# Gate and up of two experts in chunks of 1024 columns instead of 512

## The chip, the core and the metric

The kernel runs on one core of one Trainium2 chip. The metric is the time of one execution on the device in microseconds. On the core, TensorE (PE in the profile) multiplies matrices, VectorE (DVE) and ScalarE (ACT) do the elementwise work, GpSimd (POOL) does a little of it, and SyncE (SP) issues nearly all transfers from memory; 16 DMA engines carry them. Each engine works through its own queue in order.

## What is computed

A trunk of two layers over 256 tokens of width 1024 in float32: attention in three groups of heads, then a dense SwiGLU in the first layer and eight experts, two for each token, in the second. The change concerns the experts alone:

```python
logits = xf @ w_router
top_logit, top_idx = lax.top_k(logits, 2)
gates = softmax(top_logit)
# for each token and each of its two experts e:
y = (silu(x @ w_gate[e]) * (x @ w_up[e])) @ w_down[e]
out = h + sum of gates * y
```

w_gate and w_up of an expert are 1024 x 3584, w_down is 3584 x 1024: 44.0 MB for each expert, 352 MB for all eight. Every expert's weights are read once.

## The kernel before

The first 500 us or so are attention, the dense layer and the router. Then the experts run. The kernel counts the tokens of each expert and sorts experts 1 to 7 by count; expert 0 keeps its place. When all but three have at most 32 tokens, as here, the path `woven()` runs. It holds two streams:

- **Heavy (H):** three experts whose weights are split on the way, since a product in float32 is made of three products in a faster format. ACT makes the high part of a group of weights (`whi`, line 124), DVE the rest (`wlo`, line 125), and `mm3` (lines 238 to 240) multiplies high by high, high by low and low by high. Expert 0 and the expert with place 2 in the order have up to 128 tokens, one tile: `large_one` does these two, and the change is in there. The expert with place 1 has two tiles: `large_two`, lines 1348 to 1350.
- **Small (S):** five experts with at most 32 tokens each. TensorE multiplies their weights as they are (lines 1442 for gate and up, 1464 for down). A group is one row block of 1792 columns (896 KB) or two rows of down (1024 KB); an expert has 32 groups of the first kind and 14 of the second, 46 in all.

A heavy group is 512 KB: [128, 2, 512] of gate or up, which is two rows of 2 KB on each of 128 partitions, or [128, 1, 1024] of down, one row of 4 KB. Gate and up are cut into seven chunks of 512 columns. Each chunk takes four groups of gate, four of up, and then four groups of down of the chunk before; `turn` transposes the chunk's product of 512 columns through one PSUM bank (line 1290), and ACT and DVE split the result (lines 1293 and 1294). One expert has 84 heavy groups.

A string `order` fixes in which order the groups of the two streams are loaded and used: some 30 heavy groups are loaded before `woven()` starts, and then 0.3 small groups go beside each heavy group of the one-tile experts, and 2.1 beside each of the two-tile expert. `fill()` issues the loads on SP (line 79) in this order whenever a raw buffer is free. A heavy group frees its raw buffer when its split is done, a small group when its matmuls are done. There are five slots for split weights; `LOOK = 3` says how far ahead in the order the splits are issued.

In PSUM, `gu` has two banks: gate of a chunk goes to the first, up to the second. ACT reads gate for SiLU (line 1312), DVE multiplies it with up (line 1310). `wide_y` holds the sums of down. One bank, `tr`, serves all transposes and gathers. `jobs` is a list of small pieces of work (one-hot matrices, gathers, adding an expert's result back); one is taken after each group of the order. In chunk `NCH - 2`, the last but one, the gather of the next expert's rows is hung on this list: `gather`, lines 845 to 880, whose one-hot matrix lies in the tile `ph`, of which there is one. `gather_few` (lines 1405 and 1410) does the same for a small expert through the same tile. The instructions of each engine are put in order by a scheduler when the kernel is built, so the order in the trace is not line by line that of the code.

Of the kernel before, what the change touches and what calls it, by code (L numbers as in the profile page):

```python
# [8 lines left out]
F32 = mybir.dt.float32  # L9
# [3 lines left out]
AF = mybir.ActivationFunctionType  # L13
ALU = mybir.AluOpType
# [4 lines left out]
KT = D // 128  # L19
# [21 lines left out]
def encoder_kernel(ctx: ExitStack, tc: tile.TileContext, a: dict, consts: bass.AP, out: bass.AP):  # L41
    nc = tc.nc
# [15 lines left out]
    groups = []  # L58
# [5 lines left out]
    pos_ = {"dma": 0, "split": 0, "use": 0, "end": 1 << 30, "most": 1 << 30, "large": False}  # L64
# [131 lines left out]
    n_dense = len(groups)  # L196
    def expert_groups(e, chunks, pairs=False, by_columns=False):


        wg, wu = ([v.rearrange("e (k p) n -> p (e k) n", p=128) for v in (a[nm][0, bass.ds(e, 1)],)][0]  # L200
                  for nm in ("w_gate_moe", "w_up_moe"))
        wd = a["w_down_moe"][0, bass.ds(e, 1)].rearrange("e (k p) n -> p (e k) n", p=128)
        res = []
        for i, c in enumerate(chunks):
            c0 = c * 512
            ks = range(0, KT, 2)
            order = [(w, k) for k in ks for w in (wg, wu)] if pairs else [(w, k) for w in (wg, wu) for k in ks]
            both = [w[:, k:k + 2, c0:c0 + 512] for w, k in order]
            before, this = ([wd[:, k:k + 1, :] for k in range(4 * b, 4 * b + 4)] for b in (c - 1, c))
            last = c == chunks[-1]  # L210
            if by_columns and last:
                this = [wd[:, 4 * c:4 * c + 4, k:k + 256] for k in range(0, D, 256)]
                both, before = before, both
            res += both + (before if i else []) + (this if last else [])
        return res

    def wide_groups(e, parts, by_columns=False):


        wg, wu = (a[nm][0, bass.ds(e, 1)].rearrange("e (k p) n -> p (e k) n", p=128)  # L220
                  for nm in ("w_gate_moe", "w_up_moe"))
        wd = a["w_down_moe"][0, bass.ds(e, 1)].rearrange("e (c p r) n -> p (e c) r n", p=128, r=WR)
        res = []
        for c in parts:
            res += [w[:, k:k + 1, c * WIDE:(c + 1) * WIDE] for k in range(KT) for w in (wg, wu)]
            ends = WR - 4 if by_columns and c == parts[-1] else WR
            res += [wd[:, c, r:r + 2, :] for r in range(0, ends, 2)]
            if ends < WR:
                res += [wd[:, c, ends:, k:k + 256] for k in range(0, D, 256)]
        return res  # L230

    WIDE, WR = DFE // 2, DFE // 256
    NCH = DFE // 512
    groups += expert_groups(0, list(range(NCH)))

    def mm3(ps, xs, ws, start, stop):
        (xh, xl), (wh, wl) = xs, ws
        nc.tensor.matmul(ps, xh, wh, start=start, stop=False)  # L238
        nc.tensor.matmul(ps, xh, wl, start=False, stop=False)  # L239
        return nc.tensor.matmul(ps, xl, wh, start=False, stop=stop).ins  # L240
# [29 lines left out]
    def gcol(base, l, k):  # L270
        return gt[:, base + 8 * l + k:base + 8 * l + k + 1]
# [434 lines left out]
    def moe():  # L706
        with ExitStack() as st:
            mp = st.enter_context(tc.tile_pool(name="moe", bufs=1, reuse_waits="tile"))
# [58 lines left out]
            for k in range(KT):  # L767
# [3 lines left out]
                d, g = hTs[k // 4][:, k % 4, :], gcol(G_FFN, 1, k)  # L771
# [147 lines left out]
            for t in range(NT):  # L919
                last = nc.scalar.activation(gate[:, t, :], gate[:, t, :], AF.Exp, scale=rs[:, t:t + 1])  # L920
# [177 lines left out]
            def result():  # L1098
                y = psum.tile([128, 2, 512], F32, name="y", bufs=1)
                return [y[:, q, :] for q in range(2)]  # L1100
# [113 lines left out]
            def woven():  # L1214
# [5 lines left out]
                        released(i)  # L1220
                loaded = pos_["dma"]
                few = [7, 6, 5, 3, 4]
                heavy = groups[n_dense:n_dense + 24 * NCH] + [g for c in every for g in expert_groups(ids[0], [c])]
                assert pos_["use"] == n_dense
                small = [g for e in few for g in wide_groups(ids[e - 1], [0, 1], e == few[-1])]
                order = "H" * (loaded - pos_["use"])
                n_h, n_s, due = len(order), 0, 0.0
                while n_h < len(heavy):
                    due += 0.3 if n_h < 24 * NCH else 2.1
                    order += "H"  # L1230
                    n_h += 1
                    while due >= 1.0:
                        order += "S"
                        n_s += 1
                        due -= 1.0
# [6 lines left out]
                n_split, n_used = [pos_["split"] - base], [0]  # L1242
                ready = dict(spl)

                def split_next():
                    i = n_split[0]
                    pos_["split"] = at[i]
                    hi, lo = split_into(at[i], slots[(at[0] - n_dense + i) % len(slots)])
                    ready[at[i]] = hi, lo
                    n_split[0] += 1  # L1250

                def take_heavy():
                    i = pos_["use"]
                    assert order[i - base] == "H"
                    while i not in ready:
                        split_next()
                    pos_["use"] += 1
                    return ready.pop(i)
# [9 lines left out]
                gu = [psum.tile([128, 512], F32, name="gu", bufs=2) for _ in range(2)]  # L1268
                wide_y = result()
                fixed.append(bank)  # L1270
                n, m = WIDE // 4, 256
# [11 lines left out]
                def large_one(col, slot, after):  # L1283

                    x, ths = xs[slot], None

                    def turn(hc):
                        pt = tr().rearrange("p (f c) -> p f c", f=4)
                        for f in range(4):
                            nc.tensor.transpose(pt[:, f, :], hc[:, f * 128:(f + 1) * 128], ident)  # L1290
                        th = mp.tile([128, 4, 128], F32R, name="th", bufs=2)
                        tl = mp.tile([128, 4, 128], F32R, name="tl", bufs=2)
                        nc.scalar.activation(th, pt, AF.Copy)
                        nc.vector.tensor_tensor(tl, pt, th.bitcast(F32), op=ALU.subtract)
                        return th, tl

                    for c in [*every, NCH]:
                        if c < NCH:
                            hc = mp.tile([128, 512], F32, name="sg", bufs=2)
                            for v in range(2):  # L1300
                                for kg in range(4):
                                    yield
                                    w = take_heavy()
                                    for k in range(2):
                                        kk = kg * 2 + k
                                        mm3(gu[v], (x[0][:, kk, :], x[1][:, kk, :]), (w[0][:, k, :], w[1][:, k, :]),
                                            kk == 0, kk == KT - 1)
                                    n_used[0] += 1
                                if v:
                                    nc.vector.tensor_tensor(hc, gu[v], hc, op=ALU.mult)  # L1310
                                else:
                                    nc.scalar.activation(hc, gu[v], AF.Silu)
                            if c == 1:
                                jobs.append(lambda: turn_hot(one_hot(col, cm[:, :128]), phTs[slot]))
                            if c == NCH - 2:
                                jobs.extend(after)
                        if c:
                            for f in range(4):
                                yield
                                wh, wl = take_heavy()  # L1320
                                for q in range(2):
                                    sl = slice(q * 512, q * 512 + 512)
                                    mm3(wide_y[q], (ths[0][:, f, :], ths[1][:, f, :]), (wh[:, 0, sl], wl[:, 0, sl]),
                                        c == 1 and f == 0, c == NCH and f == 3)
                                n_used[0] += 1
                        if c < NCH:
                            ths = turn(hc)
                    take(wide_y, spare(slot))
                    later_combine(col, slot, spare(slot))

# [195 lines left out]
            for dst, v in ((posS, pos), (gateS, gate)):  # L1526
# [3 lines left out]
            every = list(range(NCH))  # L1530
            ids = nc.values_load_multi_w_load_instructions(regs[0:1, 1:8], engines=[mybir.EngineType.SP],
                                                           min_val=0, max_val=NE - 1)[1]
# [158 lines left out]
```

## Time and profile before

| | us |
|---|---|
| median of 3 runs | 1404.87 (1404.04 to 1405.04) |
| the profiled execution | 1403.66 |
| its span, from first to last instruction | 1401.9 |
| PE busy | 1305.1 (93%) |
| DVE busy | 787.8 (56%) |
| ACT busy | 614.7 (44%) |

427.9 MB are moved, 305 GB/s over the span. Busy time of PE is modelled at its ends, since matmuls overlap; the start times are exact. The share of DMA is the mean busy share of the 16 engines; it can stand a little above 1, since a packet can begin before the last has ended. TensorE's clock is given as a share of full speed.

### The profile page before, as it was taken

To read this page: it belongs to the slowest core of one execution; us is meant where nothing else is said; L and a number is where in the kernel's file an instruction comes from. 1 tells how busy PE (TensorE), PEld (TensorE's weight loads), DVE (VectorE), ACT (ScalarE), POOL (GpSimd) and SP (SyncE) were. 2 spreads that over 40 slices of the span, in tenths; PEclk is the share of its full clock that TensorE was granted. 3 is DMA by queue.
4 is the path that set the end of the run, shared out by engine and by line. 5 is a ranking of instruction groups with operands and counts; after the bars stand their busy time and mean duration, and the time that the engine had idled before them with its cause. 6 is when DMAs were issued, how large, how long until landed. Compare 5 with 4: busy or idle time off the path is not lost.

```text
span 1401.9 us, 21803 instructions
## 1 busy us (share of the span) xinstructions
PE 1305.1 (93%) x8247; PEld 943.9 (67%) x8247; DVE 787.8 (56%) x1332; ACT 614.7 (44%) x951; POOL 70.2 (5%) x58
## 2 busy tenths in 40 slices
PE   8999999999999889999999989898999898989886
PEld 8886888888986567675666656565656566555642
DVE  7877877754986778675766553333332233233333
ACT  8576665643676556654555442212131212122211
POOL 0300011100300500000000000000000000000000
PEclk9999999999999999999999999999999999999999
DMA  8631555555654748999999987999999999999994
GB/s 269 188 120 64 178 181 180 185 193 163 209 173 151 267 164 306 377 405 375 379 402 403 357 327 293 361 411 415 410 416 410 416 411 414 412 414 413 413 418 163
DMA packets 146486, 427.87 MB, mean 305 GB/s; under 512 B 10412, under 2 KB 55860, under 8 KB 137668
## 3 DMA queue, kind: packets, MB, share of 16 engines
q1 hardware_dynamic: 146000, 425.62, 80.3%
q8 instruction: 66, 1.08, 0.3%
q0 software_dynamic: 288, 0.74, 0.2%
q14 instruction: 48, 0.39, 0.1%
q10 hardware_dynamic: 84, 0.04, 0.0%
HBM read 425.31 MB, written 1.05 MB: 304 GB/s over the span
## 4 chain that ended last, share of the span: by engine, by line
PE 66%; DMA 19%; DVE 9%; issue 2%; ACT 2%; POOL 1%; SPq 0%; ACTq 0%; DVEq 0%; POOLq 0%
DMA rawm<-in_w_down_moe_dram 8%; PE acc L652 6%; PE cb L1442 6%; PE y L239 3%; PE acc L238 3%; DMA room<-in_w_down_moe_dram 3%; PE acc L239 3%; PE acc L240 3%; PE y L238 3%; PE y L240 3%; PE gu L238 3%; PE acc L653 3%; PE gu L239 3%; PE gu L240 3%; PE tr L1464 3%; DVE wlo L125 2%
## 5 line engine op out<-in xcount | busy, mean ns | idle before, releaser
L140 DVE TENSOR_TENSOR wlo<-raw,whi 128x1024 fp32r<-128x1024 f32 (+2 forms) x134 | 149.0, 1115 | 58.2 <-ACT whi L139 58.0
L139 ACT ACTIVATE whi<-raw 128x1024 fp32r<-128x1024 f32 (+2 forms) x140 | 133.9, 966 | 75.2 <-PE acc L240 56.7
L125 DVE TENSOR_TENSOR wlo<-rawm,whi 128x1024 fp32r<-128x1024 f32 x87 | 104.8, 1220 | 68.6 <-ACT whi L124 68.6
L652 PE MATMUL acc<-u,whi 128*128 128x512 f32 x352 | 124.7, 399 | 0.0
L124 ACT ACTIVATE whi<-rawm 128x1024 fp32r<-128x1024 f32 x87 | 89.8, 1053 | 56.2 <-DMA rawm<-in_w_gate_moe_dram 19.3
L1349 PE MATMUL gu<-x,wlo 128*128 128x256 f32 x360 | 102.8, 290 | 10.8 <-DVE wlo L125 10.8
L1348 PE MATMUL gu<-x,whi 128*128 128x256 f32 x360 | 100.6, 296 | 5.3 <-ACT whi L124 5.3
L1350 PE MATMUL gu<-x,whi 128*128 128x256 f32 x360 | 100.7, 284 | 0.0
L653 PE MATMUL acc<-u,wlo 128*128 128x256 f32 x352 | 98.9, 281 | 0.0
L1348 PEld LDWEIGHTS gu<-x,whi 128*128 128x128 f32 x360 | 65.7, 190 | 31.6 <-issue 17.2
L238 PE MATMUL gu<-whi,x 128*128 128x512 f32 x178 | 73.7, 414 | 6.4 <-DVE regs L1525 4.6
L1349 PEld LDWEIGHTS gu<-x,wlo 128*128 128x128 f32 x360 | 68.5, 190 | 14.7 <-DVE wlo L125 13.7
L238 PE MATMUL acc<-whi,u 128*128 128x384 f32 (+1 forms) x224 | 75.4, 337 | 2.9 <-ACT qk_dil L566 2.9
L652 PEld LDWEIGHTS acc<-u,whi 128*128 128x128 f32 x352 | 66.2, 188 | 16.4
L240 PE MATMUL acc<-whi,u 128*128 128x384 f32 (+1 forms) x224 | 74.2, 331 | 0.0
L239 PE MATMUL acc<-wlo,u 128*128 128x384 f32 (+1 forms) x224 | 74.2, 331 | 0.0
L239 PE MATMUL gu<-wlo,x 128*128 128x512 f32 x178 | 72.2, 405 | 1.8 <-DVE wlo L125 1.6
L240 PE MATMUL gu<-whi,x 128*128 128x512 f32 x178 | 71.0, 399 | 0.0
L1350 PEld LDWEIGHTS gu<-x,whi 128*128 128x128 f32 x360 | 68.6, 191 | 0.5 <-issue 0.5
L1442 PE MATMUL cb<-rawm,room 128*32 128x448 f32 x528 | 67.1, 553 | 0.0
L653 PEld LDWEIGHTS acc<-u,wlo 128*128 128x128 f32 x352 | 66.5, 189 | 0.0
L125 DVE TENSOR_TENSOR wlo<-room,whi 128x1024 fp32r<-128x1024 f32 x25 | 30.5, 1222 | 45.3 <-ACT whi L124 45.3
(404 smaller groups left out, 2921.6 us busy)
## 6 DMA issues: line engine op xcount, KB each, us to landing
rawm<-in_w_up_moe_dram SPq DMA_DIRECT2D x35, 896.0 KB, 15.7
rawm<-in_w_gate_moe_dram SPq DMA_DIRECT2D x31, 896.0 KB, 14.9
rawm<-in_w_down_moe_dram SPq DMA_DIRECT2D x26, 1024.0 KB, 15.4
rawm<-in_w_down_moe_dram SPq DMA_DIRECT2D x48, 512.0 KB, 9.4
raw<-in_w_down_moe_dram SPq DMA_DIRECT2D x22, 1024.0 KB, 16.0
raw<-in_w_gate_moe_dram SPq DMA_DIRECT2D x23, 896.0 KB, 14.9
rawm<-in_w_up_moe_dram SPq DMA_DIRECT2D x36, 512.0 KB, 10.4
raw<-in_w_up_moe_dram SPq DMA_DIRECT2D x20, 896.0 KB, 15.7
```

What stands on the lines that cost most here:

```text
L125: nc.vector.tensor_tensor(xl, x, xh.bitcast(F32), op=ALU.subtract)
L139: nc.scalar.activation(xh, x, AF.Copy)
L140: (engine or nc.vector).tensor_tensor(xl, x, xh.bitcast(F32), op=ALU.subtract)
L238: nc.tensor.matmul(ps, xh, wh, start=start, stop=False)
L239: nc.tensor.matmul(ps, xh, wl, start=False, stop=False)
L240: return nc.tensor.matmul(ps, xl, wh, start=False, stop=stop).ins
L652: nc.tensor.matmul(ps, wh[:, k, fs], u[:, k], start=k == 0, stop=False)
L653: nc.tensor.matmul(ps[:, 0, :], wl[:, k, fs], uh[:, k, :], start=False, stop=k == KT - 1)
L1348: nc.tensor.matmul(o, wh, xh, start=kk == 0 and f % 2 == 0, stop=False)
L1349: nc.tensor.matmul(o, wl, xh, start=False, stop=False)
L1350: nc.tensor.matmul(o, wh, xl, start=False, stop=kk == KT - 1 and f % 2 == 1)
L1442: done = nc.tensor.matmul(ps[sub[j], :n], xr[:, k, :], v[:, 0, j * n:j * n + n], start=k == 0, stop=k == KT - 1)
```

## The change

The two one-tile experts take gate and up in chunks of up to 1024 columns. Expert 0 has its first three chunks as before, since their groups are loaded by the code in front of `woven()`, and then two of 1024; the other has three of 1024 and one of 512. A group of a wide chunk is [128, 1, 1024], one row of 4 KB on each partition, and covers one block of 128 rows of the contraction. Within a wide chunk, gate fills both `gu` banks (columns 0 to 511 and 512 to 1023), SiLU is taken from both, then up fills the same two banks. Down of a wide chunk takes eight groups. A wide chunk is transposed by two calls of `turn`. The gather of the next expert's rows is hung on the last chunk. The number of groups, their bytes and the order of H and S stay as they are.

```diff
+    def one_groups(e, chunks):
+        wg, wu, wd = (a[nm][0, bass.ds(e, 1)].rearrange("e (k p) n -> p (e k) n", p=128)
+                      for nm in ("w_gate_moe", "w_up_moe", "w_down_moe"))
+        res, last = [], []
+        for c0, n in chunks:
+            step = 1024 // n
+            res += [w[:, k:k + step, c0:c0 + n] for w in (wg, wu) for k in range(0, KT, step)] + last
+            last = [wd[:, k:k + 1, :] for k in range(c0 // 128, (c0 + n) // 128)]
+        return res + last
...
-                heavy = groups[n_dense:n_dense + 24 * NCH] + [g for c in every for g in expert_groups(ids[0], [c])]
-                assert pos_["use"] == n_dense
+                cut = {0: [(0, 512), (512, 512), (1024, 512), (1536, 1024), (2560, 1024)],
+                       2: [(0, 1024), (1024, 1024), (2048, 1024), (3072, 512)]}
+                heavy = one_groups(0, cut[0]) + one_groups(ids[1], cut[2])
+                n_one = len(heavy)
+                heavy += [g for c in every for g in expert_groups(ids[0], [c])]
+                assert pos_["use"] == n_dense and loaded <= n_dense + 36
...
-                    for c in [*every, NCH]:
-                        if c < NCH:
-                            hc = mp.tile([128, 512], F32, name="sg", bufs=2)
+                    chunks = cut[col]
+                    for c in range(len(chunks) + 1):
+                        if c < len(chunks):
+                            halfs = chunks[c][1] // 512
+                            hc = [mp.tile([128, 512], F32, name="sg", bufs=2) for _ in range(halfs)]
                             for v in range(2):
-                                for kg in range(4):
-                                    yield
-                                    w = take_heavy()
-                                    for k in range(2):
-                                        kk = kg * 2 + k
-                                        mm3(gu[v], (x[0][:, kk, :], x[1][:, kk, :]), (w[0][:, k, :], w[1][:, k, :]),
+                                for kk in range(KT):
+                                    if halfs == 2 or kk % 2 == 0:
+                                        yield
+                                        w = take_heavy()
+                                    for i in range(halfs):
+                                        wh, wl = (u[:, kk % (3 - halfs), i * 512:i * 512 + 512] for u in w)
+                                        mm3(gu[i if halfs == 2 else v], (x[0][:, kk, :], x[1][:, kk, :]), (wh, wl),
                                             kk == 0, kk == KT - 1)
-                                    n_used[0] += 1
-                                if v:
-                                    nc.vector.tensor_tensor(hc, gu[v], hc, op=ALU.mult)
-                                else:
-                                    nc.scalar.activation(hc, gu[v], AF.Silu)
+                                    if halfs == 2 or kk % 2:
+                                        n_used[0] += 1
+                                for i in range(halfs):
+                                    if v:
+                                        nc.vector.tensor_tensor(hc[i], gu[i if halfs == 2 else 1], hc[i], op=ALU.mult)
+                                    else:
+                                        nc.scalar.activation(hc[i], gu[i], AF.Silu)
...
-                            if c == NCH - 2:
+                            if c == len(chunks) - 1:
                                 jobs.extend(after)
                         if c:
-                            for f in range(4):
+                            for f in range(4 * len(ths)):
                                 yield
                                 wh, wl = take_heavy()
+                                th, tl = (u[:, f % 4, :] for u in ths[f // 4])
...
-                        if c < NCH:
-                            ths = turn(hc)
+                        if c < len(chunks):
+                            ths = [turn(v) for v in hc]
```

## Rows read from the trace of the kernel before

**Rows 1.** Windows by stage: stretch, length, busy us by engine, PEclk, DMA share, GB/s

```profile
505.00:560.00 55.00, 55.00 (x257) 44.57 (x259) 44.92 (x45) 39.43 (x42) 0.00 (x0) 0.97 0.80 285
570.00:640.00 70.00, 70.00 (x366) 48.09 (x364) 48.78 (x47) 43.46 (x46) 0.00 (x0) 1.00 1.03 403
640.00:690.00 50.00, 45.86 (x234) 28.23 (x231) 33.34 (x36) 24.17 (x30) 0.00 (x0) 1.00 0.99 370
690.00:790.00 100.00, 95.68 (x497) 63.76 (x496) 65.25 (x65) 53.61 (x61) 0.00 (x0) 1.00 1.03 400
790.00:860.00 70.00, 62.72 (x375) 43.28 (x373) 36.63 (x40) 25.49 (x31) 0.00 (x0) 0.93 0.78 302
900.00:1370.00 470.00, 423.67 (x3322) 271.46 (x3318) 153.01 (x170) 104.46 (x129) 0.00 (x0) 0.98 1.02 413
```

**Rows 2.** Timeline of one chunk: start us, us, engine, line, operation [idle before <-releaser]

```profile
702.67 0.39 PE L238 MATMUL gu<-wlast,x 128*128 128x512 f32 x1
702.90 0.40 PE L239 MATMUL gu<-wlast,x 128*128 128x512 f32 x1
...
708.54 0.39 PE L240 MATMUL gu<-whi,x 128*128 128x512 f32 x1
708.96 0.60 ACT L1312 ACTIVATE sg<-gu 128x512 f32<-128x512 f32 x1 [4.34 <-PE gu L240]
...
717.21 0.60 PE L1290 MATMUL tr<-cs,sg 128*128 128x128 f32 x4
718.34 1.05 ACT L124 ACTIVATE wlast<-raw 128x1024 fp32r<-128x1024 f32 x1
718.48 0.69 DVE L1294 TENSOR_TENSOR tl<-tr,th 128x512 fp32r<-128x512 f32 x1 [0.88 <-ACT th L1293]
...
719.01 0.96 PE L1442 MATMUL cb<-rawu,room 128*32 128x448 f32 x8
```

**Rows 3.** Short windows, columns as in rows 1, and packets of two of them

```profile
704.00:708.00 4.00, 4.00 (x29) 2.59 (x29) 2.01 (x2) 0.62 (x1) 0.00 (x0) 1.00 1.04 392
758.00:760.00 2.00, 2.00 (x11) 1.61 (x10) 0.80 (x1) 0.11 (x1) 0.00 (x0) 1.00 1.05 388
718.00:720.00 2.00, 2.00 (x14) 0.81 (x12) 1.27 (x2) 2.00 (x3) 0.00 (x0) 1.00 1.02 409
744.00:746.00 2.00, 2.00 (x14) 0.80 (x13) 2.00 (x2) 2.00 (x3) 0.00 (x0) 1.00 1.01 406
...
DMA packets 810, 1.57 MB, mean 392 GB/s; under 512 B 47, under 2 KB 47, under 8 KB 810
...
DMA packets 223, 0.82 MB, mean 409 GB/s; under 512 B 24, under 2 KB 24, under 8 KB 223
```

**Rows 4.** Timeline of SP: issues at heavy places 33, 53, 85 and 140

```profile
511.29 0.38 SPq L79 DMA_DIRECT2D rawu<-in_w_gate_moe_dram  x1
...
562.49 0.42 SPq L79 DMA_DIRECT2D rawm<-in_w_down_moe_dram  x1
...
623.17 0.39 SPq L79 DMA_DIRECT2D rawh<-in_w_gate_moe_dram  x1
...
741.66 0.33 SPq L79 DMA_DIRECT2D rawm<-in_w_down_moe_dram  x1
```

**Rows 5.** DMA issues of the whole span: count, KB each, median us to landing

```profile
rawm<-in_w_gate_moe_dram SPq DMA_DIRECT2D x28, 512.0 KB, 10.1
```

**Rows 6.** Timeline, 765 to 781 us: first and last matmuls of the second expert's gather

```profile
765.20 0.60 PE L874 MATMUL tr<-ph,hg 128*128 128x128 f32 x4
...
779.53 1.38 PE L874 MATMUL tr<-ph,hg 128*128 128x128 f32 x10
```

**Rows 7.** Timeline around 799 us, and the window 797 to 805

```profile
794.70 4.32 PE L1410 MATMUL tr<-ph,hg 128*128 128x32 f32 x32
...
799.06 0.35 DVE L866 TENSOR_SCALAR ph<-io,posS,rs 128x128 f32<-128x128 f32 x1 [6.33 <-PE tr L1410]
...
797.00:805.00 8.00, 7.01 (x26) 5.61 (x26) 5.94 (x7) 1.06 (x1) 0.00 (x0) 0.57 0.66 226
```

More of the change, by code (lines that the diff above doesn't have):

```diff
@@ L1228, in woven @@
                 while n_h < len(heavy):
-                    due += 0.3 if n_h < 24 * NCH else 2.1
+                    due += 0.3 if n_h < n_one else 2.1
                     order += "H"
@@ L1321, in large_one @@
                                 for q in range(2):
                                     sl = slice(q * 512, q * 512 + 512)
-                                    mm3(wide_y[q], (ths[0][:, f, :], ths[1][:, f, :]), (wh[:, 0, sl], wl[:, 0, sl]),
-                                        c == 1 and f == 0, c == NCH and f == 3)
+                                    mm3(wide_y[q], (th, tl), (wh[:, 0, sl], wl[:, 0, sl]), c == 1 and f == 0,
+                                        c == len(chunks) and f == 4 * len(ths) - 1)
```

## The prediction

> **What bounds the kernel now.** I read the windows by stage first, then the DMA queue in short windows, then the timeline at the places that the change touches. The windows [rows 1] cut the expert stage into parts. From 570 to 640 us and from 690 to 790 us the 16 DMA engines are busy the whole time (share 1.03) and move 403 and 400 GB/s: weights arrive as fast as they can, and TensorE waits for them. From 640 to 690 the share is 0.99 at 370 GB/s, because the first expert ends there. From 790 to 860 it falls to 0.78 at 302 GB/s: the second one-tile expert ends, its sums are split and added back, and the rows of the two-tile expert are gathered. From 900 to 1370 the share is 1.02 at 413 GB/s. So after the dip at 790 to 900 the end is set by bytes that the change doesn't touch. What the change saves or loses before 900 goes to the end one for one, if the dip doesn't take it.
>
> Busy PE counts for little as a measure here, because ends of matmuls are modelled. The starts tell more: matmuls of 512 columns follow each other every 0.23 us [rows 2], so a heavy group of weights (six of them, three for each half) is 1.40 us of TensorE. A group of the small experts is about 0.96 us [rows 2], and the order puts 0.3 of them beside each heavy group: 1.40 + 0.3 x 0.96 = 1.69 us. The DMA time of the same mix is (0.524 + 0.3 x 0.957) MB at 400 GB/s = 2.03 us (one small expert is 44.0 MB in 46 groups). TensorE has 0.34 us to spare per heavy group, 8 us in the 24 groups of a chunk of 1024.
>
> **The rows of weights.** Two heavy groups of [128, 2, 512] become two of [128, 1, 1024]: the same bytes, the same count, half as many rows of twice the length. Gate and up have 16 such groups in each chunk of 1024: 32 in the first expert (its last two chunks), 48 in the other (three chunks); 80 of 168 heavy groups. What a row length is worth is read from windows in which almost nothing else is in flight [rows 3]. From 704 to 708 us there are 810 packets, 47 of them tiny, for 1.57 MB, so 2 KB each: 392 GB/s. From 758 to 760 it is 388. From 718 to 720 it is 223 packets, 24 of them tiny, for 0.82 MB, so 4 KB each (down): 409 GB/s; from 744 to 746, 406. I take 390 against 407.5, which is 4.5%.
>
> The down rows lie one behind the other in memory, and the new gate rows lie 14 KB apart. The small experts' gate and up rows have this same pitch, and the stretches made mostly of their long rows still reach 413 GB/s [rows 1], so I see no charge for the pitch.
>
> Not all 80 groups lie where DMA is the limit. Counted along SP's issues of 512 KB, chunk 1536 to 2560 of the first expert takes the places of the heavy groups 33 to 48, issued from 511 us on [rows 4], in a stretch whose share is only 0.80 [rows 1]: there a faster transfer only waits earlier. The next chunk begins at place 53, issued at 562 us, and the second expert's three chunks run from place 85 at 623 us to place 140 at 742 us [rows 4]. That is 16 + 48 = 64 groups, 33.6 MB, in saturated time: 33.6 MB at 390 GB/s is 86.0 us, at 407.5 GB/s 82.3 us. **Gain 3.7 us.** The bounds: nothing, if the pitch costs what the length saves; and 5.1 us, from the packets' own times: a share of 1.04 of 16 engines over 4 us for 763 packets is 87 ns a packet, 1.02 over 2 us for 199 is 164 ns [rows 3]; 2 x 87 - 164 = 10 ns, times 8192 pairs, over 16 engines. I take the rate, since a share above 1 shows that short packets overlap.
>
> The Trainium skill, DMA: Bandwidth & Descriptors (Specifications), asks for at least 512 B per transfer for line rate, by which 2 KB rows would have nothing to gain; the trace disagrees, with 390 against 407.5 GB/s. The same page (Why small descriptors are slow) gives a fixed overhead of about 3 cycles per packet beside 32 B per beat: 67 beats twice against 131 is an estimate of 2.2%, and the sum would be 1.9 us by it.
>
> **The new order on TensorE.** Before, gate has one bank and up the other, and neither waits for its reader within a chunk. Now gate fills both banks and up reuses them.
> - Gate to up: SiLU on ACT starts at 708.96, 0.42 us after the bank's last matmul began, and takes 0.60 us [rows 2]. The bank is free 1.02 us after that matmul's start; up needs it after four starts, 0.93 us. That is 0.1 us of waiting, and at most 2.2 us when two splits of 1.05 us [rows 2] stand ahead in ACT's queue. Behind the waiting matmul stand TensorE's own next groups, and the raw buffers of the small experts that they free.
> - Up to the next gate: two products on DVE, hidden by the 8 down groups (11 us) of the chunk before. Where there is no chunk before, the transposes needed the products already.
> - Two turns in a row share one bank: transposes at 717.21, then a copy on ACT, then the difference on DVE from 718.48 to 719.17 [rows 2]. The second set can start 1.96 us after the first, not 0.60: 1.4 us of waiting, five times in all.
> SiLUs, products, copies and transposes stay the same in number. The new waits are 1.5 to 3.6 us per chunk of 1024, against 8 us to spare, and a transfer in the queue needs about 10 us to land [rows 5], so a pause of that size doesn't drain the queue. I cost them at **nothing** in the saturated stretches. If TensorE were the limit there, five chunks would cost 7.5 to 18 us. The first of the five starts near the end of the unsaturated stretch and may cost its 1.5 us.
>
> **What is moved.** The gather of the next expert's rows was hung on the last chunk but one, and is now hung on the last. For the first expert that is place 68 instead of 64, nearly the same. For the second it is place 156 instead of 148, with 12 groups left to the expert's end instead of 20. Before, its matmuls filled gaps between 765 and 781 us [rows 6], under a full DMA queue, so for nothing. Its new place is the stretch from 790 to 860, where DMA is not full. Its cost there: 32 matmuls, 10 of them in 1.38 us [rows 6], so 4.4 us of TensorE at most if nothing else is idle, and nothing if all of it falls into the 7 us in which TensorE idles there anyway [rows 1]. Before, it was spread thin in gaps; I take **+1.0 us**. DVE's part brings more risk: the one tile that holds the one-hot matrix passes from user to user. At 799 DVE had waited 6.33 us for 32 matmuls of the small experts' gather that took 4.32 us [rows 7], with splits of weights behind it, and TensorE's clock fell to 0.57 of full speed, between 1.2 and 2.4 GHz, in 797 to 805 [rows 7].
>
> **Sum.** -3.7 + 0 + 1.0 = -2.7 us. The profiled execution took 1403.7 us (span 1401.9 and 1.8 around it), 1.2 us under the median of 1404.9. So 1401.0 us there, and **1402.2 us** as a median, 0.19% less.
>
> **The rivals.**
> - The order around the second expert's end gets worse. The gather lands beside the small experts' gather and the two-tile gather, and each hands the one-hot tile on only when the other's matmuls are done. Price: 4.4 us of TensorE and one more wait such as the 6.33 us on DVE, 10.7 us, less the 3.7 us gained: up to +7 us, 1412 us, and 1408 if half of it is hidden. It decides as soon as more than 3.7 us of this falls into 790 to 860. For it: the share of 0.78, so nothing covers there. Against it: the down groups before the last turn are now 8, not 4, so there is work to fill with. Chance 0.23.
> - The dip gets shallower. The writer that blocked DVE at 793 to 799 was the two-tile gather's, sent ahead; with another gather before it, it can't run there, and splits pass. That gives back up to 6.3 us: 1404.9 - 3.7 - 6.3 = 1394.9, and 1398 if half. Chance 0.17.
> - The row length is not what the rate hangs on (the down rows are quick because they follow each other): no gain, 1405 to 1406 us. That is also where the skill's 512 B would put it. For it: only rows of down show 4 KB. Against it: the 413 GB/s of long rows at the same pitch. Chance 0.10.
> - The forecast itself, 1400 to 1404.5 us, 0.50.
>
> A measurement can tell about 0.2% of this kernel, 2.8 us: faster is below 1402.1, slower above 1407.7. The forecast's case lies across the lower border, half on each side: faster 0.25 + 0.17 = 0.42, the same 0.25 + 0.10 = 0.35, slower 0.23. The range that leaves 2 in 10 out reaches into both outer cases: 1396 to 1410 us. The likeliest case's own range is 1400 to 1404.5.
>
> **What would show it.** Right: windows full of gate and up of the second expert at 405 to 410 GB/s, a share still at 1.0 or more from 570 to 790, the two-tile expert's loads some 3 us earlier. The waits: TensorE's first up matmul of a chunk after SiLU, and the second turn after DVE's difference, each near 1 to 2 us. Wrong: a share below 1 between 690 and 790 (the new waits do reach the queue), a rate that stays at 390, or a lost time between 790 and 900 that differs from before by more than 3 us.

## The result, and the profile after

| | before | after |
|---|---|---|
| median, us | 1404.95 (1404.04 to 1405.14, 4 runs) | 1395.96 (1395.45 to 1396.95, 4 runs) |
| the profiled execution's span, us | 1401.9 | 1393.7 |

The ratio is 0.9938, with a 95% interval of 0.9921 to 0.9955: about 9 us less (6 to 11 by the interval), where 2.7 had been forecast. The windows by stage of the kernel after answer [rows 1], column by column (stretch, length, busy us by engine, PEclk, DMA share, GB/s):

```profile
505.00:560.00 55.00, 55.00 (x259) 43.78 (x257) 45.05 (x44) 39.41 (x42) 0.00 (x0) 0.97 0.80 285
570.00:640.00 70.00, 70.00 (x357) 46.68 (x356) 48.04 (x45) 39.96 (x43) 0.00 (x0) 1.00 1.02 408
640.00:690.00 50.00, 47.49 (x238) 29.77 (x238) 33.55 (x35) 25.36 (x30) 0.00 (x0) 1.00 0.94 358
690.00:790.00 100.00, 97.17 (x503) 64.03 (x503) 68.27 (x66) 56.59 (x63) 0.00 (x0) 1.00 1.02 409
790.00:860.00 70.00, 65.78 (x432) 45.89 (x431) 34.95 (x42) 25.70 (x35) 0.00 (x0) 0.98 0.84 329
900.00:1362.00 462.00, 421.23 (x3275) 272.91 (x3276) 149.37 (x167) 101.43 (x126) 0.00 (x0) 0.97 1.02 413
```

The rate rose where long rows came in: 408 for 403 and 409 for 400 GB/s. But between 640 and 690 it fell, 358 for 370, with the share at 0.94 for 0.99. And from 790 to 860, the dip is shallower: share 0.84 for 0.78, clock 0.98 for 0.93.

Windows made mostly of the new rows of gate and up answer [rows 3], with the packets of the first of them:

```profile
730.00:734.00 4.00, 4.00 (x25) 2.50 (x24) 3.71 (x4) 2.33 (x3) 0.00 (x0) 1.00 1.03 416
716.00:718.00 2.00, 2.00 (x10) 1.39 (x8) 2.00 (x3) 1.51 (x2) 0.00 (x0) 1.00 1.01 409
...
DMA packets 419, 1.66 MB, mean 416 GB/s; under 512 B 48, under 2 KB 48, under 8 KB 419
```

By the sizes of their packets they hold 324 and 163 rows of 4 KB, and the groups that land next are gate and up of the second expert; 47 and 21 rows of 7 KB, of the small experts, run among them and may lift the rate a little. So rows of 4 KB that lie 14 KB apart run about as fast as the rows of down did, 406 and 409 [rows 3].

Where did the 9 us come from? Two lines of the view of a source line tell it: the matmuls of the two one-tile experts, with the start of the first and the last one behind the three durations (minimum, median, maximum in ns). Before:

```profile
L238 PE MATMUL gu<-whi,x x178: 390/395/767, 504.4 to 817.6; 128*128 128x512 f32 x178
L238 PE MATMUL y<-whi,th x92: 387/393/774, 528.8 to 837.9; 128*128 128x512 f32 x92
```

and after, in the same view:

```profile
L249 PE MATMUL gu<-whi,x x178: 387/395/763, 503.5 to 799.3; 128*128 128x512 f32 x178
L249 PE MATMUL y<-whi,th x92: 392/393/628, 527.7 to 829.1; 128*128 128x512 f32 x92
```

From the first start of gate to the last of down it is 837.9 - 504.4 = 333.5 us before and 325.6 after. From there to the end of the span it is 1401.9 - 837.9 = 564.0 and 564.6 us. In all twelve kernels of this text this last stretch is 563.9 to 564.9 us. The prediction said that bytes set it, and there the splits do wait for landings: 138 us of ACT's waits between 900 and 1362 us of the kernel before end on a DMA, the longest rows being

```profile
ACT whi L124 <- DMA room<-in_w_down_moe_dram: 21.0, 5, 4.8
ACT whi L124 <- DMA rawm<-in_w_gate_moe_dram: 19.3, 4, 5.1
```

That fits; no run lengthened either side of this stretch. Ahead of the first start the code is the same in all twelve, and yet it comes between 503.5 and 508.1 us: single executions differ there by more than some of the effects below, so traces are compared from that start on. What the change does, it does while the one-tile experts run. Counted along TensorE's starts, heavy places 1 to 137 take 255.1 us before and 254.8 after, and places 137 to 168, **the end of the second one-tile expert, take 77.0 us before and 69.4 after**. The whole gain from the first start on lies in the last 32 of 168 heavy groups.

The work at that end in the trace after, from the timeline (start us, us, engine, line, operation, idle before and releaser), which answers [rows 6] and [rows 7]:

```profile
788.18 1.38 PE L885 MATMUL tr<-ph,hg 128*128 128x128 f32 x10
...
795.23 1.38 PE L885 MATMUL tr<-ph,hg 128*128 128x128 f32 x10
...
802.71 3.54 PE L1432 MATMUL tr<-ph,hg 128*128 128x32 f32 x30
...
806.74 0.60 DVE L877 TENSOR_SCALAR ph<-io,posS,rs 128x128 f32<-128x128 f32 x2 [3.74 <-PE tr L1432]
```

The gather that was moved runs in six pieces between 785 and 797 us, two of them with ten matmuls, where it ran in seven between 765 and 781 before. The scheduler puts it ahead of the place at which it is hung: its matmuls stand at places 139 to 144 before and 151 to 155 after. DVE's wait for the small experts' gather is 3.74 us for 6.33.

### The profile page after: what moved, and what is told of

Its sections match the earlier page's. It is cut to its first block, busy times and chain, and to the rows that moved or that the text cites. A ratio compares the mean times of both kernels' runs of the same rounds, so it can differ in the third digit from the quotient of the medians.

```text
span 1393.7 us, 21809 instructions
## 1 busy us (share of the span) xinstructions
PE 1307.1 (94%) x8247; PEld 944.9 (68%) x8247; DVE 786.9 (56%) x1332; ACT 614.3 (44%) x951; POOL 71.4 (5%) x58
## 3 DMA queue, kind: packets, MB, share of 16 engines
HBM read 425.31 MB, written 1.05 MB: 306 GB/s over the span
## 5 line engine op out<-in xcount | busy, mean ns | idle before, releaser
L249 PE MATMUL gu<-whi,x 128*128 128x512 f32 x178 | 69.1, 416 | 5.3 <-issue 4.6
L251 PE MATMUL gu<-whi,x 128*128 128x512 f32 x178 | 70.7, 397 | 0.0
```

## The experiments

Three explanations stood against each other at first. **Rows**: the longer rows bring bytes sooner, as forecast, and more of them than I had counted. **End**: the order around the second expert's end, which the moved gather sets, made the dip shallower. **Chunks**: the wider chunks themselves help TensorE, in one expert or in both. Each part can be undone or done alone.

**Short rows in the kernel after.** The order of the chunks stays, but each wide group is loaded as two rows of 2 KB:

```diff
-            res += [w[:, k:k + step, c0:c0 + n] for w in (wg, wu) for k in range(0, KT, step)] + last
+            res += [w[:, k:k + 2, x:x + 512] for w in (wg, wu) for k in range(0, KT, 2) for x in range(c0, c0 + n, 512)] + last
...
-                                        wh, wl = (u[:, kk % (3 - halfs), i * 512:i * 512 + 512] for u in w)
+                                        j = i if halfs == 2 else kk % 2
+                                        wh, wl = (u[:, j, :] for u in w)
```

> The changed kernel with its 80 wide groups loaded as [128, 2, 512], rows of 2 KB as before; the same bytes in all, but a group's two halves are two rows of 512 instead of one of 1024, so gate and up are multiplied in a wrong pairing. All else stays: chunks, banks, order, gather. Theory R (the row length is worth some 4 us, the order of the work the other 5): 4 us slower than the changed kernel, about 1400 us, windows of the second expert back at 400 GB/s. Theory O (the order is worth all 9 us, faster rows only wait earlier): 1396 us. Theory L (the rows are worth all 9 us): 1405 us.

Measured: 1396.86 us (1395.11 to 1398.7, 5 runs) against 1404.97 before; ratio 0.9949 (0.9936 to 0.9963). All of the gain but about 1 us is there without a long row of gate or up in the two experts, and this interval overlaps that of the kernel after. The last down group starts as in the kernel after (source view, then the window from 690 to 790):

```profile
L249 PE MATMUL y<-whi,th x92: 392/393/628, 528.0 to 829.4; 128*128 128x512 f32 x92
...
690.00:790.00 100.00, 97.18 (x503) 63.77 (x502) 68.49 (x66) 56.59 (x63) 0.00 (x0) 1.00 1.03 403
```

The rate is 403 here and 409 in the kernel after, and TensorE is at the same place at the same time.

**Long rows in the kernel before.** The reverse: the order of before, and the same 80 groups loaded with 4 KB rows:

```diff
+                        for b in range(2):
+                            at_ = first + (0 if c + b == 0 else 8 + 12 * (c + b - 1))
+                            heavy[at_:at_ + 8] = [v[:, k:k + 1, c * 512:c * 512 + 1024] for v in (wg, wu)
+                                                  for k in range(b * 4, b * 4 + 4)]
```

> The kernel before with the gate and up groups of the same chunks loaded as [128, 1, 1024], rows of 4 KB; the same bytes, chunks of 512 in two banks as before, so again a wrong pairing. Theory R: 4 us faster than before, 1401 us, the dip from 790 us as deep as before (some 9 us of idle DMA between 790 and 830). Theory O: 1405 us. Theory L: 1396 us.

Measured: 1405.41 us (1402.91 to 1408.05, 11 runs) against 1404.97; ratio 1.0005 (0.9996 to 1.0014). Windows and source view of this kernel:

```profile
570.00:640.00 70.00, 70.00 (x364) 48.86 (x361) 49.37 (x46) 43.32 (x46) 0.00 (x0) 1.00 1.02 412
640.00:690.00 50.00, 45.94 (x225) 28.29 (x224) 32.15 (x35) 22.51 (x28) 0.00 (x0) 1.00 0.94 359
...
L238 PE MATMUL gu<-whi,x x178: 388/394/767, 508.1 to 821.3; 128*128 128x512 f32 x178
L238 PE MATMUL y<-whi,th x92: 392/393/774, 532.5 to 841.6; 128*128 128x512 f32 x92
```

The rows do what the forecast said, 412 for 403 GB/s, and the time doesn't move. From the first start to the last it is 841.6 - 508.1 = 333.5 us, to the tenth what it was before. What came sooner lay in the buffers, and DMA then stood idle longer (share 0.94 for 0.99 from 640 to 690). The two runs together leave at most about 1 us of **Rows**, and nothing that either interval tells from zero.

**The gather where it was.** The kernel after, with the second expert's gather hung at place 148 again:

```diff
-                            if c == len(chunks) - 1:
+                            if c == len(chunks) - 1 and not col:
                                 jobs.extend(after)
...
+                            if c == len(chunks) - 2 and col:
+                                jobs.extend(after)
```

> The changed kernel with the second expert's gather hung on the list at heavy place 148, where it was before, instead of 156. Theory G (the later place of the gather makes the dip shallower, since the gather and not the two-tile gather follows on the one-hot tile): 4 to 5 us slower than the changed kernel, 1400 to 1401 us, and DVE again waits about 6 us for the small experts' gather. Theory C (the dip is shallower because of the wide chunks: more down groups and an earlier last gate and up): within 1 us of the changed kernel, 1396 us. If my step in the prediction was right (a later place costs 1 us): 1395 us.

**The gather alone.** The kernel before, with it hung at place 156:

```diff
+                                if c == NCH - 1 and not v and col:
+                                    jobs.extend(after)
...
-                            if c == NCH - 2:
+                            if c == NCH - 2 and not col:
```

> The kernel before with the second expert's gather hung at heavy place 156 instead of 148. Theory G: 4 to 5 us faster than before, 1400 us. Theory C: 1405 us, or 1406 by the prediction's step.

Measured: without the move 1400.24 us (1397.91 to 1403.64, 9 runs), ratio 0.9963 (0.9947 to 0.9978); with the move alone 1399.86 us (1396.73 to 1400.88, 5 runs), ratio 0.9965 (0.9952 to 0.9979); both against 1404.97. So each of the two does about half: 1405.0 before, 1400.2 with the wide chunks alone, 1399.9 with the move alone, 1396.0 with both. The stretch from place 137 to 168 on TensorE, in windows, first of before and then of the kernel after:

```profile
761.00:838.00 77.00, 70.01 (x362) 48.02 (x361) 44.34 (x47) 35.06 (x41) 0.00 (x0) 0.93 0.90 348
```

```profile
760.00:829.00 69.00, 66.10 (x362) 45.84 (x361) 42.97 (x46) 32.23 (x38) 0.00 (x0) 0.98 0.94 373
```

then of the kernel without the move, and of the one with the move alone, each with DVE's wait for the small experts' gather from the view of waits (waiting operation and releaser: us in total, times, longest):

```profile
760.00:833.00 73.00, 67.95 (x363) 47.50 (x362) 43.59 (x46) 32.59 (x38) 0.00 (x0) 0.95 0.90 352
...
DVE ph L877 <- PE tr L1434: 5.4, 1, 5.4
```

```profile
761.00:832.00 71.00, 66.10 (x365) 45.07 (x364) 44.93 (x47) 34.62 (x41) 0.00 (x0) 1.00 0.95 375
...
DVE ph L866 <- PE tr L1412: 3.5, 1, 3.5
```

The same number of matmuls (362 to 365) takes 77, 73, 71 and 69 us. The clock is 0.93, 0.95, 1.00 and 0.98 of full speed. TensorE's idle time, length less busy, is 7.0, 5.1, 4.9 and 2.9 us. Each window is one execution, and that of the move alone ran 2.0 us under its median.

What the old place of the gather costs can be read from two starts, those of places 137 and 148. Between them the kernel before does the gather, and the one with the move alone does the same eleven heavy groups without it. First before, then the move alone:

```profile
760.18 0.40 PE L238 MATMUL y<-whi,th 128*128 128x512 f32 x1
787.46 0.51 PE L238 MATMUL gu<-whi,x 128*128 128x512 f32 x1
```

```profile
760.62 0.40 PE L238 MATMUL y<-whi,th 128*128 128x512 f32 x1
783.97 0.50 PE L238 MATMUL gu<-whi,x 128*128 128x512 f32 x1
```

That is 27.3 and 23.4 us, both at a clock of 1.00: 3.9 us for the gather.

**One expert at a time.** First the second expert as in the kernel after, the first as before; then the reverse, with the second one's gather at place 148:

```diff
-                cut = {0: [(0, 512), (512, 512), (1024, 512), (1536, 1024), (2560, 1024)],
+                cut = {0: [(i * 512, 512) for i in range(7)],
...
-                            if c == len(chunks) - 1:
+                            if c == len(chunks) - (2 if len(chunks) == NCH else 1):
```

> Expert 0 as in the kernel before (seven chunks of 512, gather at place 64), the second one-tile expert as in the changed kernel. Theory P (the time is set by TensorE's progress to the last heavy group of the second expert, place 168, and the whole gain arises between places 137 and 168; expert 0's wide chunks cost TensorE 1 us): 1395 us, or 1 us below the changed kernel. If the wide chunks of both experts bring the gain in equal parts (fewer chunk ends): 1400 to 1401 us.

```diff
-                       2: [(0, 1024), (1024, 1024), (2048, 1024), (3072, 512)]}
+                       2: [(i * 512, 512) for i in range(7)]}
...
-                            if c == len(chunks) - 1:
+                            if c == len(chunks) - (2 if len(chunks) == NCH else 1):
```

> Expert 0 as in the changed kernel (three chunks of 512, two of 1024), the second expert as before, its gather at place 148. Theory P: 1405 to 1406 us, no gain. Equal parts: 1400 to 1401 us.

Measured: the second alone 1394.69 us (1392.42 to 1395.53, 5 runs), ratio 0.9922 (0.9909 to 0.9935); the first alone 1405.70 us (1402.3 to 1408.55, 12 runs), ratio 1.0002 (0.9993 to 1.0012); both against 1405.28. The change to expert 0 brings nothing. On TensorE its wide chunks cost 1 us: places 33 to 81 take 95.0 us in the kernel after, 94.0 before. The version with the second expert alone has the lowest median of all, 1394.69, but its interval overlaps that of the kernel after, so that it is better is not shown.

**The writer that held DVE up.** My rival had explained the shallower dip by DVE's wait: the two-tile gather's one-hot write, sent ahead, waits for the tile `ph`, and splits of weights wait behind it [rows 7]. To test it, the two-tile gather is held back until the second expert's sums are split, first in the order of before, then in that of after:

```diff
+                    ended.append(take(wide_y, spare(slot)))
...
+                    with tc.issue_after(ended[-1]):
+                        gather(1, CAP, 2, tr)
```

> The kernel before, but the two-tile gather's instructions on DVE are queued behind the last split of the second expert's sum, so that its write of the one-hot tile can't stand in DVE's queue at 793 to 799 us with splits of weights behind it. Theory D (that wait on DVE, 6.33 us, is what the later gather takes away): 2 to 5 us faster than before, 1400 to 1403 us. Theory K (what counts is the order of the matmuls on TensorE and its clock, which falls after the small experts' gather): 1405 us, within 1 us.

> The changed kernel with the same hold on the two-tile gather's instructions on DVE; there DVE waited 3.7 us for the small experts' gather. Theory D: 1 to 2 us faster than the changed kernel, 1394 to 1395 us. Theory K: 1396 us.

Measured: in the order of before 1402.13 us (1400.25 to 1404.24, 8 runs), ratio 0.9976 (0.9966 to 0.9986), so 3.2 us less (2.0 to 4.8); in the order of after 1395.92 us (1395.11 to 1396.98, 5 runs), ratio 0.9933 (0.992 to 0.9946), as without it. Holding the write back is thus worth some 3 us in the old order, about a third of the 9 us, and nothing in the new one: the first is what Theory D expected, the second what Theory K did. That the 3 us are DVE's wait is not shown. The window of the first of these from 761 to 838 us:

```profile
761.00:838.00 77.00, 70.93 (x364) 48.81 (x363) 44.54 (x45) 34.83 (x41) 0.00 (x0) 0.93 0.89 346
```

In this trace the wait is gone, the matmuls come in the same order as before and the clock is as low, and yet places 137 to 168 take 76.4 us for 77.0: in place of the wait DVE waits longer for ACT's high parts (14.3 us for 8.4 between 755 and 860). The profiled execution was the slowest of the eight, 1404.24 us, so the trace doesn't show where the 3.2 us of the medians went.

**Who waits for whom.** Rows had fallen, so the statement that TensorE waits for weights from 570 to 790 had to be tested from both sides. Rows of 1 KB make DMA slower; 20 more matmuls of 512 columns, whose results are overwritten, make TensorE longer by 20 x 0.23 = 4.7 us:

```diff
+                        heavy[at_:at_ + 8] = [v[:, k:k + 4, x:x + 256] for v in (wg, wu) for k in (0, 4)
+                                              for x in (c * 512, c * 512 + 256)]
```

> The kernel before with the same 80 gate and up groups loaded as [128, 4, 256], rows of 1 KB; the same bytes, multiplied in a wrong pairing. From 87 ns for 2 KB and 164 ns for 4 KB a row of 1 KB would take some 48 ns, 338 GB/s against 390, so 42 MB take 16 us more of the DMA engines. Theory W (TensorE waits for weights, my prediction's step): 13 to 16 us slower than before, 1418 to 1421 us. Theory P (TensorE's own progress is the limit up to 838 us, and DMA has idle time to spend, 21 us of it between 790 and 900): much less, 1405 to 1409 us.

```diff
+                                    for _ in range(5 if col and 0 < c < 5 and not v and not kg else 0):
+                                        nc.tensor.matmul(gu[v], x[0][:, 0, :], w[0][:, 0, :], start=True, stop=True)
```

> The kernel before with 20 more matmuls of 512 columns, whose results are thrown away: five ahead of gate in each of the second expert's chunks 1 to 4, between 690 and 760 us, where the DMA engines are busy all the time. They are 20 x 0.233 = 4.7 us of TensorE. Theory W (TensorE has 8 us to spare per 1024 columns there): within 1 us of before, 1405 us. Theory P: 4 to 5 us slower, 1409 to 1410 us.

Measured: with 1 KB rows 1402.99 us (1401.55 to 1407.3, 11 runs), ratio 0.9991 (0.9981 to 1.0002), no loss, and below even the range of Theory P; with more matmuls 1408.44 us (1406.26 to 1411.21, 12 runs), ratio 1.0025 (1.0014 to 1.0037), which is 3.5 us of the 4.7, with an interval from 2.0 to 5.2; both against 1405.09. The stretch from 570 to 790 and the last starts, first with 1 KB rows and then with more matmuls:

```profile
570.00:790.00 220.00, 211.48 (x1093) 140.09 (x1091) 147.50 (x146) 120.52 (x135) 0.00 (x0) 1.00 1.05 384
...
L238 PE MATMUL y<-whi,th x92: 392/393/774, 527.7 to 835.6; 128*128 128x512 f32 x92
```

```profile
570.00:790.00 220.00, 212.45 (x1085) 141.78 (x1084) 144.19 (x140) 118.35 (x134) 0.00 (x0) 0.99 1.01 388
...
L238 PE MATMUL gu<-whi,x x178: 388/395/767, 505.4 to 824.1; 128*128 128x512 f32 x178
L238 PE MATMUL y<-whi,th x92: 387/393/774, 530.4 to 843.2; 128*128 128x512 f32 x92
```

In the first, DMA moves 384 GB/s with its queue full, and TensorE keeps its pace (835.6 less a first start of 503.5: 332.1 us), though ACT's splits now wait 4.5 us for landings. In the second, from first to last start it is 843.2 - 505.4 = 337.8 us, 4.3 more than before, and DMA falls to 388 GB/s although its rows are as before: **the transfers follow TensorE, not TensorE the transfers**. The stock has an end, though: 1 KB rows bring (394 - 384) GB/s x 220 us = 2.2 MB less than before in this stretch, about four groups of 512 KB, and were still in time. A longer stretch might not be; no run here shows it.

## Why the prediction went as it did

The time came out at 1395.96 us, at the very edge of the range (1396, with 0.04 us between them) and far below the likeliest case (1400 to 1404.5), in the place of the rival "the dip gets shallower" (1394.9 to 1398), to which I had given 0.17. That the kernel became faster, as forecast, is luck: the one term that was to bring it, the rows, brought nothing that can be measured, and the two that brought it stood in the sum at nothing and at a loss.

- **The step that failed: "weights arrive as fast as they can, and TensorE waits for them."** The full queue from 570 to 790 [rows 1] was real; that somebody waited for it was not. In these 220 us of the kernel before, the view of waits has for TensorE two rows on a DMA, 0.8 us in all:

```profile
PEld cb L1442 <- DMA raw<-in_w_down_moe_dram: 0.4, 1, 0.4
PEld cb L1442 <- DMA rawm<-in_w_up_moe_dram: 0.4, 1, 0.4
```

  ACT and DVE, whose splits TensorE needs, have no row on a DMA at all there. [rows 1] had it too: PE is busy 70.00 of 70.00 us and 95.68 of 100. I set that aside because ends of matmuls are modelled, and went by a sum of starts, 1.69 us of TensorE for each heavy group against 2.03 us of DMA. The sum was too short. From all starts of matmuls between 570 and 790, each up to the next, the 109 heavy groups take 171.5 us, 1.57 each and not 1.40, since some starts come late, after a split or a wait; the small experts take 32.4 us, 0.30 each, as I had it; gathers, turns and adding back take 16.1 us, 0.15 each, which I had left out. That is 2.02 us. From start to start the pieces have to fill the stretch whatever limits it, so this sum alone proves nothing; what it tells is that 0.15 us of work and 0.17 us of late starts stand where I had counted 0.34 us to spare, and the two tests above tell that TensorE, not DMA, held the pace. A queue stays full as long as raw buffers come free, and here TensorE's pace freed them.
- **The rows.** Their rate was about right: 409 and 416 GB/s, with some longer rows among them, where 407.5 had been taken. Over 570 to 790 it is 397 GB/s in the kernel after and 394 before. Their 3.7 us were worth nothing in time, as the run with long rows alone shows (1405.41 for 1404.97 us). The rule of the Trainium skill that I had weighed (DMA: Bandwidth & Descriptors, Specifications: 512 B are enough) is contradicted in the rate by these rows. The estimate worked out from the same page's 3 cycles per packet (Why small descriptors are slow), 2.2%, is too low here: 409 GB/s against 388 to 392 [rows 3] is 4 to 5%. The rival without a gain from the rows was right about the time and wrong about why: the rate rises, but TensorE sets the time.
- **The new waits on TensorE.** Their sizes were right. At one chunk of the kernel after, the timeline has:

```profile
751.52 0.60 ACT L1333 ACTIVATE sg<-gu 128x512 f32<-128x512 f32 x1 [5.14 <-PE gu L251]
752.17 0.50 PE L249 MATMUL gu<-whi,x 128*128 128x512 f32 x1 [0.21 <-ACT sg L1333]
752.17 0.19 PEld L249 LDWEIGHTS gu<-whi,x 128*128 128x128 f32 x1 [0.66 <-ACT sg L1333]
...
773.79 0.69 DVE L1310 TENSOR_TENSOR tl<-tr,th 128x512 fp32r<-128x512 f32 x1 [3.25 <-ACT th L1309]
774.54 0.65 PE L1306 MATMUL tr<-cs,sg 128*128 128x128 f32 x4 [0.29 <-DVE tl L1310]
```

  and the view of waits from 570 to 790:

```profile
PEld gu L249 <- ACT sg L1333: 4.3, 8, 0.7
```

  The wait for SiLU is 0.2 us at the matmul and 0.66 at the load of its weights, between the 0.1 and the 2.2 of the bounds, and 4.3 us in eight such loads, part of which lies under the matmuls before. The second turn does wait for DVE's difference, but the scheduler put other groups in between, and 0.29 us of idle time is left. What failed is why they should cost nothing: not a slack on TensorE hides them, since there is none. Places 33 to 81, with both wide chunks of expert 0, take 95.0 for 94.0 us, the next eight 21.5 for 22.7, and up to place 137 nothing is lost. So they cost some 1 us in passing, against the 7.5 to 18 that I had priced for the case that TensorE is the limit.
- **The moved gather.** Forecast +1.0 us, measured -5.1 alone in the order of before, and -4.3 in that of after (1400.24 to 1395.96, the medians of before beside them being 0.02 apart). The sign was wrong. I took its old place for free "under a full DMA queue"; with TensorE as the limit its 32 matmuls cost 3.9 us there. The price of the new place was fair: places 151 to 158 take 21.0 us with the gather in the move alone, and 23.2 before without it, of which at most 3.4 us (8 x 0.43 [rows 7]) are the lower clock. So it costs there 1.2 us at most.
- **The wide chunks of the second expert.** I gave them nothing but the rows; they bring about 4.7 us without the move (1400.24 against 1404.97), and with the move short rows do as well as long ones (1396.86). My own remark, that 8 groups of down stand ahead of the last turn and not 4, fits with this, since the gain lies in places 137 to 168. That these groups are the reason is argued, not shown.
- **The rival that came true** was right in what it said of the trace, a shorter wait of DVE and a dip less deep. As a mechanism it is at most a part: the held write is worth 3.2 us in the old order by the medians and 0.6 in the trace, while 3.9 us lie ahead of 790, at the gather's old place.
- **A slip in a rival's sum.** In "gets worse", half of 10.7 us less 3.7 is 1.7 us and gives 1406.5 us, not 1408. Nothing hung on it.

**What stays open** is how the 7.6 us from place 137 to 168 divide. Three things change together there: DVE's wait (6.3, 5.4, 3.5, 3.7 us in before, without the move, move alone, after), TensorE's idle time (7.0, 5.1, 4.9, 2.9), and its clock, which was at its lower level, 1.2 GHz, in parts of this stretch. Three pairs of traces in which all matmuls from place 137 to 168 come in the same order give the clock a price. The kernel after and the one with the second expert alone agree to some 0.01 us up to place 158; there the first falls to the lower level and the second does not:

```profile
802.71 3.54 PE L1432 MATMUL tr<-ph,hg 128*128 128x32 f32 x30
...
808.20 0.63 PE L251 MATMUL y<-whi,tl 128*128 128x512 f32 x1
...
812.12 0.39 PE L249 MATMUL y<-whi,th 128*128 128x512 f32 x1
```

```profile
803.40 3.54 PE L1432 MATMUL tr<-ph,hg 128*128 128x32 f32 x30
...
811.87 0.39 PE L249 MATMUL y<-whi,th 128*128 128x512 f32 x1
```

From the small experts' gather to the same matmul it is 9.4 us in the first and 8.5 in the second: this drop costs 0.9 us. The kernel with 1 KB rows has the order of before without the drop at 825 us and is 1.2 us shorter from place 137 to 168; the one with the first expert alone has half of the drop at 798 us and is 0.8 us shorter. The other half of that drop can cost at most the 1.7 us that it takes from full speed (half of 8 x 0.43 [rows 7]). So the clock costs 2.0 to 3.7 us before and 0.9 after, which makes it 1.1 to 2.8 of the 7.6 us. DVE's wait alone is worth 0.6 us at the same clock (the held write). The rest, some 4 to 6 us, is the order of the work: the gather's old place for one part, and for the other the wide chunks, by which 8 down groups stand ahead of the last turn; in the two traces that stay at 1.00, the move alone and the second expert alone, the wide chunks are worth 1.8 us (70.3 for 68.5). How the whole divides between these, and whether idle time and a lower clock bring each other, no run here shows. A one-hot tile of its own for the two-tile gather, which would remove DVE's wait in any order, wasn't tried.

## What to carry to other kernels

A DMA share of 1 says that the queue is never empty, not that anyone waits for what it brings: look for the engine whose waits end on a landing, and look also at the engines that feed it (here the splits on ACT), and when there is none, lengthen either side by a known amount (slower rows, some dead matmuls) and see which the time follows. A sum by which an engine has time to spare has to hold everything that the engine does in the stretch, small gathers and transposes too, and what is then missing against the pace of its starts has to be found in its waits. Where side work is hung near the end of a phase it can weigh more than the rate of the loads: here four to five microseconds for eight places, 3.9 of them for 32 matmuls taken to be free.

## What the runs showed of the hardware

- Shorter rows cost less than I had expected. From 570 to 640 us, with the queue full in each kernel, the stretch moves 387 GB/s with 1 KB rows in the 80 groups (share 1.05), 403 with 2 KB (1.03, [rows 1]) and 412 with 4 KB (1.02): a quarter of the row length costs 6% in this mix, in which the small experts' rows and down are unchanged.
- The same matmuls at the same distances can meet either level of the clock. The kernel after and the one with the second expert alone agree to some 0.01 us from place 137 to 158, with the 32 matmuls of 32 columns each at its end; then the first shows matmuls of 512 columns every 0.43 us (1.2 GHz), eight in a row, and the second keeps 0.23 us (2.4 GHz), but for one wait of 0.35 us for a split. The drop cost 0.9 us.
- In the kernel before, the granted clock of 0.57 in 8 us [rows 7] begins while the 32 matmuls of 32 columns run, during which TensorE did nothing else for 4.32 us. Its second drop, 0.66 from 824 to 829 us, has none of them ahead of it but a turn with 0.5 us of waiting for ACT, and the kernel with 1 KB rows runs the same order there at 1.00. So neither is shown to be the cause.
